# Raw weights asked for one chunk sooner, and a stick pair's first sigmoids and scan put behind the last begun weight chunk

## The chip, the cores and the metric

The kernel runs on one core of one Trainium2 chip. The metric is the device time of one execution in microseconds (us). The engines that matter here: TensorE (PE) multiplies, with its weight loads shown as PEld; VectorE (DVE) and ScalarE (ACT) work on elements; GpSimd (POOL) does little here but issue some transfers; SyncE (SP) only issues DMA transfers. Each of these takes its instructions in the order in which they were built, and waits in place where one is not ready.

## The reference

One decoder layer for a sequence of 512 tokens of width 1024, all in float32. Cut to what matters:

```python
h = rms_norm(x, norm_w)
qa, ka, va, za, qb, kb, vb, zb, gl_a, gl_b = split(h @ w_in)     # 8 x 512 columns, 2 x 1024
oa = moba_attention(rms_norm(qa), rms_norm(ka), va, rel_bias)    # 8 heads: scores, bias, softmax, values
ob = stick_breaking_attention(qb, kb, vb)                        # 8 heads, see below
ya = (oa * silu(za)) @ w_up_moba
yb = (ob * silu(zb)) @ w_up_sb
y  = sigmoid(gl_a + b_a) * ya + sigmoid(gl_b + b_b) * yb
x  = x + y @ w_out
```

A stick-breaking head weights key s of query t with sigmoid(z_ts) times the product of (1 - sigmoid(z_tj)) over the keys j between s and t. The product is a running one along a row, and is made with a scan instruction.

## The kernel before

**Three products for one.** Each float32 operand is split into a high part, which the matmul takes at full rate, and a low rest. A product is three matmuls: low by high, high by low, high by high (`mm3`, L225 to L227). Weights come as *chunks* of 128x1024 elements (512 KB). For each chunk SP issues the transfer into a raw tile `wr` (L170); ACT copies it to the high part `wh` (L179); DVE subtracts, which gives the low part `wl` (L181). There are three raw tiles and three each of `wh` and `wl`, used in turn, so chunk c's transfer waits until chunk c-3 is split, and chunk c's split until PE has used chunk c-3.

**Which chunk when.** `load_w` hands out chunks in the order of `stream` and keeps three fetched ahead: taking chunk c writes down transfer and split of chunk c+2. In the middle of the kernel the chunks go: 43 `zb:0`, 44 `za:3`, 45 `k:2`, 46 `g:9` (a block of gate logits), 47 `zb:1`, 48 `g:10`, 49 `k:3`, 50 `zb:2`, 51 `g:11`, 52 `up:0`, 53 `zb:3`. A tile carries its chunk's number: `wl48` belongs to chunk 48. A chunk of this kind is 24 matmuls of 512 columns.

**The pairs.** The loop over `PAIRS` (m = 0 to 7) handles two heads at a time: four pairs of branch a (softmax heads 0 to 7), then four of branch b (stick heads). For pair m it computes the scores of both heads on PE (L504), the weighted sum of pair m-2 (L594, evicted by DVE as `oa`, L599, then split into `oha` and `ola`), and then, for each head, turns scores into weights and stores them; between these stand the `FILLS`, the chunks that give PE work meanwhile: three to a pair here. A softmax head (`softmax`) is a bias add and minimum on DVE (L524), four exponentials on ACT (L526), scaling on DVE, three transposes on DVE (L566), four stores to DRAM from SP (`put`, L573, `pda6` for head 6) and one load back from ACT's queue (`get`, L580). A stick head (`stick`) has, for each of three row groups, two sigmoids on ACT (`om` = 1 - weight, L541, and `pb`, L542; L550 and L551 for the short rows), a scan on DVE (`sx`, L544, L554), a product (L546, L556), then the same transposes, stores (`pdb`) and load. Results of chunks of kind g are evicted by a sigmoid on ACT (L621), kind z by a sigmoid and a product (L607, L608), kind k by a split (L412, L413). They use two banks named `pj` in turn, with the weighted sums.

**What sets the order.** A scheduler in the tile layer places the instructions of each engine from its own estimate of when they are ready; `tc.issue_after(x)` adds that a row may stand only behind row x. Before, a stick head's first sigmoids are held behind the last gate eviction:

```python
with tc.issue_after(evicted[-1]):
    A.activation(om[:, S - n:S], sc[i], AF.Sigmoid, scale=-1.0)
```

The functions that the diff touches, and what calls them:

Of the kernel before, what the change touches and what calls it, by code (L numbers as in the profile page):

```python
# [9 lines left out]
F32 = mybir.dt.float32  # L10
F32R = mybir.dt.float32r
BF16 = mybir.dt.bfloat16
AF = mybir.ActivationFunctionType
ALU = mybir.AluOpType
AX = mybir.AxisListType

P = 128
S = 512
# [40 lines left out]
def hybrid_layer(ctx: ExitStack, tc: tile.TileContext, x, xT, w, rel, out):  # L59
    nc = tc.nc  # L60
    V, A, G, T = nc.vector, nc.scalar, nc.gpsimd, nc.tensor
# [3 lines left out]
    wp = ctx.enter_context(tc.tile_pool(name="wp", bufs=3))  # L65
# [29 lines left out]
    nw, mb, qw, kw = sm[:, 0:8], sm[:, 8:24], sm[:, 24:25], sm[:, 25:26]  # L95


    ahead, low, sums = [], {}, {}
    turn_of = cp.tile([1, 1], F32, name="turn_of")
    WO = w.shape[0] - len(BLOCKS)  # L100
    ORDER = {"v": ("11", "22", "T2", "21", "T3", "T1", "T4"), "q": ("11", "T1", "21", "T2", "22", "T3", "T4")}
# [3 lines left out]
    stream = list(range(8)) + list(range(20, 20 + len(FRONT))) + VOUT + QOUT + list(range(20 + len(FRONT), WO)) + OUT  # L105

    def block(name, kind):
        if kind == "q":
            return w[BASE[kind] + BLOCKS.index(name + "a") // 2]
        return w[BASE.get(kind, WO) + BLOCKS.index(name)]  # L110
# [38 lines left out]
    count = [0]  # L149

    def load_w():

        while len(ahead) < 3 and count[0] < len(stream):
            ahead.append(fetch_w(count[0]))
            count[0] += 1
        return ahead.pop(0)

    def fetch_w(c):
        cuts = ((0, 512), (512, 1024)) if c < 2 else ((0, 1024),)
        item = stream[c]  # L160
        if item in sums:
            raw = sums[item]
        else:
            src = w[item] if isinstance(item, int) else block(item[1], item[0]) if isinstance(item, tuple) else block(item, "o")
            raw = wp.tile([P, 1024], F32, tag="wr", bufs=3, name=f"wr{c}") if c else raw0
            for a, b in cuts:
                if a == 0 and 0 < c < 4:
                    raw_x(2 * c)
                if a or c:
                    nc.sync.dma_start(raw[:, a:b], src[:, a:b])  # L170
                if a == 0 and c < 4:
                    for k in (0, 1) if c == 0 else (2 * c + 1,):
                        raw_x(k)
        hi = wp.tile([P, 1024], F32R, tag="wh", name=f"wh{c}")
        lo = wp.tile([P, 1024], F32R, tag="wl", name=f"wl{c}")
        if c == 0:
            low[c] = load_x(0)
        for a, b in cuts:
            A.activation(hi[:, a:b], raw[:, a:b], AF.Copy)  # L179
            with tc.issue_after(low[0]) if c == 0 else nullcontext():  # L180
                low[c] = V.tensor_tensor(lo[:, a:b], raw[:, a:b], hi[:, a:b].bitcast(F32), op=ALU.subtract).ins  # L181
        return hi, lo
# [6 lines left out]
    def raw_x(k):  # L189
        if k == 0:  # L190
            xraw[k] = x0[:, SM:]
            nc.sync.dma_start(x0[:, SM + P:], xT[:, SM + P:SM + S])
        else:
            xraw[k] = slot(f"xr{k}")
            nc.sync.dma_start(xraw[k], xT[:, SM + k * S:SM + (k + 1) * S])
        if k == 4:
            nc.sync.dma_start(rb, rel)

    def load_x(k):
        raw = xraw[k]  # L200
        h = xp.tile([P, S], F32R, tag="xh", name=f"xh{k}")
        l = xp.tile([P, S], F32R, tag="xl", name=f"xl{k}")
        if k == 0:
            for cs in (slice(0, P), slice(P, S)):
                V.tensor_scalar(h[:, cs], raw[:, cs], nw[:, k:k + 1], None, op0=ALU.mult)
        else:
            A.activation(h, raw, AF.Copy, scale=nw[:, k:k + 1])
        last = V.scalar_tensor_tensor(l, raw, nw[:, k:k + 1], h.bitcast(F32), op0=ALU.mult, op1=ALU.subtract)
        xH.append(h)
        xL.append(l)  # L210
        return last.ins
# [91 lines left out]
    begin = cp.tile([P, S + P + 1], F32, name="begin")  # L303
# [70 lines left out]
    def load_bias(h):  # L374
        bt = oms[h % 2][:, :S]
        nc.sync.dma_start(bt, bass.AP(tensor=e_dr.tensor, offset=e_dr.offset + h * TW, ap=[[1, P], [1, S]]))
        return bt
# [115 lines left out]
    def scores(br, p, q, k, res):  # L493

        (qh, ql), (kh, kl) = q[p], k[p]
        for grp in ((3,), (2,), (1, 0)):
            ps = [bank("s", f"s{br}{2 * p + b}{grp[0]}") for b in range(2)]
            c = 0
            for i in grp:
                n = (i + 1) * P  # L500
                for m, (x, y) in enumerate(((qh, kl), (ql, kh), (qh, kh))):
                    for b in range(2):
                        o = slice(b * HD, (b + 1) * HD)
                        T.matmul(ps[b][:, c:c + n], x[o, i * P:(i + 1) * P], y[o, :n], start=m == 0, stop=m == 2)  # L504
                for b in range(2):
                    res[2 * p + b][i] = ps[b][:, c:c + n]
                c += n
            for b in range(2):
                res[2 * p + b][grp] = ps[b][:, :c]

    def row_tiles(br, h):

        p10 = tp.tile([P, 3 * P], F32, tag="p1", bufs=2, name=f"p{br}{h}1")
        return {3: tp.tile([P, S], F32, tag="p3", bufs=2, name=f"p{br}{h}3"),
                2: tp.tile([P, 3 * P], F32, tag="p2", bufs=2, name=f"p{br}{h}2"),
                1: p10[:, :2 * P], 0: p10[:, 2 * P:], (1, 0): p10}
# [15 lines left out]
    evicted = []  # L532

    def stick(h, sc, bias):

        rows = row_tiles("b", h)
        for i in (3, 2):
            n = (i + 1) * P
            om = oms[i - 2]
            with tc.issue_after(evicted[-1]):  # L540
                A.activation(om[:, S - n:S], sc[i], AF.Sigmoid, scale=-1.0)  # L541
            A.activation(rows[i], sc[i], AF.Sigmoid)  # L542
            sx = tp.tile([P, S], F32, tag="sx", bufs=2, name=f"sx{h}{i}")
            V.tensor_tensor_scan(sx[:, n - 1::-1] if n == S else sx[:, :n][:, ::-1], om[:, S + 1 - n:][:, ::-1],  # L544
                                 begin[:, S - n:S][:, ::-1], 0.0, op0=ALU.mult, op1=ALU.add)
            V.tensor_tensor(rows[i], rows[i], sx[:, :n], op=ALU.mult)  # L546

        z, p = (a.rearrange("p (n c) -> p n c", n=3) for a in (sc[1, 0], rows[1, 0]))
        with tc.issue_after(evicted[-1]):
            A.activation(short[:, :, :P], z, AF.Sigmoid, scale=-1.0)  # L550
        A.activation(p, z, AF.Sigmoid)  # L551
        n = 3 * (P + 1) - 1
        sx = tp.tile([P, S], F32, tag="sx", bufs=2, name=f"sx{h}1")
        V.tensor_tensor_scan(sx[:, :n][:, ::-1], short.rearrange("p n c -> p (n c)")[:, 1:][:, ::-1],  # L554
                             begin[:, S + P + 1 - n:][:, ::-1], 0.0, op0=ALU.mult, op1=ALU.add)
        V.tensor_tensor(p, p, sx[:, :n + 1].rearrange("p (n c) -> p n c", n=3)[:, :, :P], op=ALU.mult)  # L556
        return rows
# [178 lines left out]
    def split_o(br, p):  # L736
        u = ocol[br, p]
        oH[br, p] = slot(f"oh{br}{p}", F32R)
        oL[br, p] = slot(f"ol{br}{p}", F32R)
        A.activation(oH[br, p], u, AF.Copy)  # L740
        V.tensor_tensor(oL[br, p], u, oH[br, p].bitcast(F32), op=ALU.subtract)
# [62 lines left out]
    def fill(tag="pj"):  # L804

        for kind, i in fills.pop(0):
            home[0] = "s" if kind == "up" else tag
            make[kind](i)
# [7 lines left out]
    def finish(m, tag="s"):  # L816

        br, p = PAIRS[m]
        weighted(tag, br, p, v_of[br], [done.pop((m, b)) for b in range(2)])
        split_o(br, p)  # L820

    for m, (br, p) in enumerate(PAIRS):
        q, k = (qa, ka) if br == "a" else (qb, kb)
        sc = {h: {} for h in (2 * p, 2 * p + 1)}
        with tc.issue_after(end[0]):
            scores(br, p, q, k, sc)
        if m > 1:
            finish(m - 2, "pj")
        for b in range(2):
            h = 2 * p + b  # L830
            bias = load_bias(h) if br == "a" else None
            done[m, b] = put(br, h, turn(br, h, (softmax if br == "a" else stick)(h, sc[h], bias)))
            fill()
            if not b:
                done[m, 0] = get(*head(m, 0), done[m, 0])
        for b in range(2):
            if not b:
                done[m, 1] = get(*head(m, 1), done[m, 1])
            if (m, b) in SUMS:
                sum_w(SUMS[m, b], done[m, b])  # L840
            fill("pj" if (b or not fills[1]) and m < 7 else "s")
# [77 lines left out]
    for c in range(2):  # L919
        hi, lo = load_w()  # L920
# [83 lines left out]
```

## Time and profile before

| | |
|---|---|
| three runs | 389.46 us median (388.74 to 389.48) |
| profiled execution | 388.84 us, of which the span of the trace 387.1 |
| PE busy | 379.2 us (98%) |
| DVE, ACT, POOL busy | 290.3, 209.0, 79.4 us |
| granted TensorE clock, mean | 0.995 |
| transfers | 86.38 MB, mean 223 GB/s |

How to read it: the profile is one execution. A row of the timeline gives start, length, engine, source line, operation and tiles; in brackets stands how long the engine was idle before and what ended that. A row of the waits gives the waiting engine and line, what released it, total time, times, and the longest. The table of stretches gives, for a stretch of time, the busy time of each engine, the granted clock, the share of DMA time and the rate. Neighbouring rows of an engine overlap by some hundredths of a microsecond, so the distance between starts is the time that one row costs.

### The profile page before, as it was taken

How to read it: one execution, taken by the hardware profiler on the slowest of the kernel's cores; microseconds unless marked ns; L12 is line 12 of the kernel's file. 1: busy time of each engine (PE TensorE's matmuls, PEld its weight loads, DVE VectorE, ACT ScalarE, POOL GpSimd, SP SyncE). 2: the span in 40 equal slices, each digit the busy share in tenths (PEclk: the TensorE clock that was granted, in tenths of full speed). 3: DMA queues.
4: the chain of work that ended last, by engine and by line, in shares of the span. 5: the costliest groups of instructions: out<-in, count | busy, mean ns of one | idle time of the engine just before them, and what ended most of it. 6: DMA issues, size and time to landing. Idle time of an engine off the chain costs nothing.

```text
span 387.1 us, 5491 instructions
## 1 busy us (share of the span) xinstructions
PE 379.2 (98%) x1935; PEld 309.3 (80%) x1935; DVE 290.3 (75%) x503; ACT 209.0 (54%) x351; POOL 79.4 (21%) x124
## 2 busy tenths in 40 slices
PE   8999999999999999999999979999999999999996
PEld 5888888888888998887878757787877887888885
DVE  5838989925767469993989396598988834999963
ACT  6685566338664448772986470654553412358540
POOL 3959959020211100000000000010101000421310
PEclk9999999999999999999999998999999999999999
DMA  7989798994854745869677734769789781499955
GB/s 269 348 325 340 198 254 255 292 331 164 225 156 108 191 127 175 238 193 318 181 224 211 253 113 117 274 205 281 253 218 307 213 316 55 143 268 295 172 141 178
DMA packets 36747, 86.38 MB, mean 223 GB/s; under 512 B 3944, under 2 KB 16744, under 8 KB 36720
## 3 DMA queue, kind: packets, MB, share of 16 engines
q1 hardware_dynamic: 27696, 52.72, 41.8%
q0 software_dynamic: 6576, 22.57, 24.2%
q10 hardware_dynamic: 2448, 10.75, 8.2%
q8 instruction: 15, 0.25, 0.3%
q14 instruction: 12, 0.10, 0.1%
HBM read 67.65 MB, written 14.70 MB: 213 GB/s over the span
## 4 chain that ended last, share of the span: by engine, by line
PE 95%; DVE 2%; DMA 1%; issue 1%; ACT 0%; DVEq 0%; ACTq 0%
PE gl L226 8%; PE gl L227 8%; PE gl L225 8%; PE pob L594 2%; PE sa L504 2%; PE za L225 2%; PE yb L225 2%; PE yb L226 2%; PE ka L225 2%; PE za L226 2%; PE yb L227 2%; PE ya L226 2%; PE za L227 2%; PE vx L227 2%; PE ka L227 2%; PE kb L227 2%
## 5 line engine op out<-in xcount | busy, mean ns | idle before, releaser
L181 DVE TENSOR_TENSOR wl<-wr,wh 128x1024 fp32r<-128x1024 f32 (+1 forms) x61 | 71.7, 1179 | 31.8 <-ACT wh L179 31.4
L179 ACT ACTIVATE wh<-wr 128x1024 fp32r<-128x1024 f32 (+1 forms) x61 | 62.7, 1028 | 45.0 <-PE ya L227 12.0
L226 PE MATMUL gl<-xh,wl 128*128 128x512 f32 x128 | 50.7, 396 | 3.2 <-DVE wl L181 3.2
L225 PE MATMUL gl<-xl,wh 128*128 128x512 f32 x128 | 50.5, 394 | 0.0
L227 PE MATMUL gl<-xh,wh 128*128 128x512 f32 x128 | 50.4, 394 | 0.0
L140 POOL COPY turn_of<-ptb 1x1 f32<-1x1 f32 x3 | 1.8, 614 | 153.7 <-DMA ptb<-pdb 153.7
L226 PEld LDWEIGHTS gl<-xh,wl 128*128 128x128 f32 x128 | 24.4, 191 | 8.6 <-DVE wl L181 3.5
L225 PEld LDWEIGHTS gl<-xl,wh 128*128 128x128 f32 x128 | 24.4, 191 | 5.4 <-issue 0.4
L227 PEld LDWEIGHTS gl<-xh,wh 128*128 128x128 f32 x128 | 24.5, 191 | 5.1
L621 ACT ACTIVATE gl<-gl,x 128x512 f32<-128x512 f32 x16 | 11.0, 687 | 30.4 <-PE gl L227 29.6
L544 DVE TENSOR_TENSOR_SCAN sx<-om,begin 128x512 f32<-128x512 f32 (+1 forms) x16 | 17.2, 1080 | 6.9 <-ACT om L541 6.9
L526 ACT ACTIVATE pa<-pa,m 128x512 f32<-128x512 f32 (+3 forms) x32 | 17.6, 552 | 1.5 <-DVE m L524 1.3
L566 DVE STREAM_TRANSPOSE turnedb<-pb 128x384 f32<-128x384 f32 (+1 forms) x24 | 13.6, 599 | 0.1
L566 DVE STREAM_TRANSPOSE turneda<-pa 128x384 f32<-128x384 f32 (+1 forms) x24 | 13.6, 597 | 0.0
L524 DVE CUSTOM_DVE_ANT_0 pa<-sa,om 128x512 f32<-128x512 f32 (+3 forms) x32 | 13.5, 484 | 0.0
L225 PE MATMUL za<-xl,wh 128*128 128x512 f32 x32 | 12.9, 403 | 0.0
L225 PE MATMUL zb<-xl,wh 128*128 128x512 f32 x32 | 12.8, 400 | 0.0
L225 PE MATMUL yb<-olb,wh 128*128 128x512 f32 x32 | 12.6, 393 | 0.0
L226 PE MATMUL zb<-xh,wl 128*128 128x512 f32 x32 | 12.5, 390 | 0.0
L226 PE MATMUL za<-xh,wl 128*128 128x512 f32 x32 | 12.5, 390 | 0.0
L226 PE MATMUL yb<-ohb,wl 128*128 128x512 f32 x32 | 12.5, 390 | 0.0
L226 PE MATMUL ka<-wh,xl 128*128 128x512 f32 x32 | 12.5, 390 | 0.0
(428 smaller groups left out, 1065.2 us busy)
## 6 DMA issues: line engine op xcount, KB each, us to landing
wr<-in_w SPq DMA_DIRECT2D x57, 512.0 KB, 5.3
pda<-turneda SPq DMA_DIRECT2D x32, 160.0 KB, 2.8
pta<-pda ACTq DMA_DIRECT2D x8, 640.0 KB, 5.1
pdb<-turnedb SPq DMA_DIRECT2D x32, 160.0 KB, 3.1
ptb<-pdb ACTq DMA_DIRECT2D x8, 640.0 KB, 4.9
qT<-in_w POOLq DMA_DIRECT2D x6, 512.0 KB, 6.3
xn<-in_x SPq DMA_DIRECT2D x8, 256.0 KB, 6.3
om<-e_dr SPq DMA_DIRECT2D x8, 256.0 KB, 3.3
```

Of the source, the lines that this page charges most:

```text
L179: A.activation(hi[:, a:b], raw[:, a:b], AF.Copy)
L181: low[c] = V.tensor_tensor(lo[:, a:b], raw[:, a:b], hi[:, a:b].bitcast(F32), op=ALU.subtract).ins
L225: T.matmul(ps, aH, bL, start=start, stop=False, skip_group_check=on)
L226: T.matmul(ps, aL, bH, start=False, stop=False, skip_group_check=on)
L227: end[0] = T.matmul(ps, aH, bH, start=False, stop=stop, skip_group_check=on).ins
L504: T.matmul(ps[b][:, c:c + n], x[o, i * P:(i + 1) * P], y[o, :n], start=m == 0, stop=m == 2)
L524: V.tensor_tensor_reduce(rows[i], sc[i], bias[:, S - n:], scale=1.0, scalar=3e38, op0=ALU.add, op1=ALU.min, accum_out=m[:, 0, i:i + 1])
L526: A.activation(rows[i], rows[i], AF.Exp, bias=m[:, 0, i:i + 1], scale=-1.0, accum_out=m[:, 1, i:i + 1])
L544: V.tensor_tensor_scan(sx[:, n - 1::-1] if n == S else sx[:, :n][:, ::-1], om[:, S + 1 - n:][:, ::-1], begin[:, S - n:S][:, ::-1], 0.0, op ...
L566: V.transpose(turned[:, :, at:at + n, :].rearrange("p q j r -> p j q r"), rows[i].rearrange("p (j q c) -> p j q c", j=n, q=4))
L594: guard[0] = T.matmul(po[o, :].rearrange("p (a n r) -> p a n r", a=4, r=32)[:, :, i:i + n, :], vv[j][:, c:c + HD], src, start=j == NT - 1, ...
L621: evicted.append(A.activation(g, ps, AF.Sigmoid, bias=mb[:, i:i + 1]).ins)
```

## The change

Two edits, and what they need.

1. `load_w` issues, from the first pair on (`early`), the raw transfer of the next chunk as soon as three are ahead; `fetch_w` then takes the raw tile from `begun`. The split stays where it was in the program.
2. In `stick`, for the first head of a pair (h even), the sigmoids are held behind the last written `wh` (`split_of[0]`) instead of behind the last gate eviction, and the first scan behind its `wl` (`split_of[1]`). `high` and `low` keep those rows.

```diff
-    ahead, low, sums = [], {}, {}
+    ahead, low, high, sums = [], {}, {}, {}
...
         while len(ahead) < 3 and count[0] < len(stream):
             ahead.append(fetch_w(count[0]))
             count[0] += 1
+        c = count[0]
+        if early[0] and c < len(stream) and isinstance(stream[c], int):
+            begun[c] = wp.tile([P, 1024], F32, tag="wr", bufs=3, name=f"wr{c}")
+            nc.sync.dma_start(begun[c], w[stream[c]])
         return ahead.pop(0)
+
+    early, begun = [False], {}
 
     def fetch_w(c):
...
             raw = sums[item]
+        elif c in begun:
+            raw = begun.pop(c)
         else:
...
         for a, b in cuts:
-            A.activation(hi[:, a:b], raw[:, a:b], AF.Copy)
+            high[c] = A.activation(hi[:, a:b], raw[:, a:b], AF.Copy).ins
...
     def stick(h, sc, bias):
 
         rows = row_tiles("b", h)
+        split_of = high[count[0] - 1], low[count[0] - 1]
         for i in (3, 2):
             n = (i + 1) * P
             om = oms[i - 2]
-            with tc.issue_after(evicted[-1]):
+            with tc.issue_after(split_of[0] if h % 2 == 0 else evicted[-1]):
                 A.activation(om[:, S - n:S], sc[i], AF.Sigmoid, scale=-1.0)
             A.activation(rows[i], sc[i], AF.Sigmoid)
             sx = tp.tile([P, S], F32, tag="sx", bufs=2, name=f"sx{h}{i}")
-            V.tensor_tensor_scan(sx[:, n - 1::-1] if n == S else sx[:, :n][:, ::-1], om[:, S + 1 - n:][:, ::-1],
-                                 begin[:, S - n:S][:, ::-1], 0.0, op0=ALU.mult, op1=ALU.add)
+            with tc.issue_after(split_of[1]) if h % 2 == 0 and i == 3 else nullcontext():
+                V.tensor_tensor_scan(sx[:, n - 1::-1] if n == S else sx[:, :n][:, ::-1], om[:, S + 1 - n:][:, ::-1],
+                                     begin[:, S - n:S][:, ::-1], 0.0, op0=ALU.mult, op1=ALU.add)
             V.tensor_tensor(rows[i], rows[i], sx[:, :n], op=ALU.mult)
...
-        with tc.issue_after(evicted[-1]):
+        with tc.issue_after(split_of[0] if h % 2 == 0 else evicted[-1]):
             A.activation(short[:, :, :P], z, AF.Sigmoid, scale=-1.0)
...
+    early[0] = True
     for m, (br, p) in enumerate(PAIRS):
```

What the scheduler makes of it. PE's rows stand as before. The lines of the changed kernel are 8 to 10 higher (L181 becomes L189, L544 becomes L554).

*First stick pair (m = 4), DVE.* `wl` is a chunk's low part, `kb2l` and `qb2l` low parts of keys and queries, `sx03` the first scan of head 0, `sx12` and `sx11` scans of head 1, `oa2` and `ola2` the evicted weighted sum. Before, the rows at the first scan, and those at `wl48`:

```order
L181 TENSOR_TENSOR wl47_2191<-wr47_2188,wh47_2190 128x1024
L413 SCALAR_TENSOR_TENSOR kb2l_2220<-kb2_2194,kb2h_2219 128x512
L413 SCALAR_TENSOR_TENSOR qb2l_2224<-qb1_1260,qb2h_2223 128x512
L544 SCALAR_TENSOR_TENSOR sx03_2314<-om1_121,begin_108 128x512
L546 TENSOR_TENSOR pb03_2310<-pb03_2310,sx03_2314 128x512
```

```order
L544 SCALAR_TENSOR_TENSOR sx12_2382<-om0_120,begin_108 128x384
L554 SCALAR_TENSOR_TENSOR sx11_2387<-om_short_116,begin_108 128x386
L546 TENSOR_TENSOR pb12_2374<-pb12_2374,sx12_2382 128x384
L181 TENSOR_TENSOR wl48_2232<-wr48_2229,wh48_2231 128x1024
L741 TENSOR_TENSOR ola2_2306<-oa2_2303,oha2_2305 128x512
L181 TENSOR_TENSOR wl49_2339<-wr49_2336,wh49_2338 128x1024
```

Now, at the first scan, and at `wl49`:

```order
L189 TENSOR_TENSOR wl47_2191<-wr47_2130,wh47_2190 128x1024
L421 SCALAR_TENSOR_TENSOR kb2l_2222<-kb2_2196,kb2h_2221 128x512
L421 SCALAR_TENSOR_TENSOR qb2l_2226<-qb1_1260,qb2h_2225 128x512
L189 TENSOR_TENSOR wl48_2232<-wr48_2194,wh48_2231 128x1024
L554 SCALAR_TENSOR_TENSOR sx03_2316<-om1_121,begin_108 128x512
L556 TENSOR_TENSOR pb03_2312<-pb03_2312,sx03_2316 128x512
```

```order
L576 STREAM_TRANSPOSE turnedb0_2329<-pb02_2313 128x3x4x32
L576 STREAM_TRANSPOSE turnedb0_2329<-pb01_2311 128x3x4x32
L554 SCALAR_TENSOR_TENSOR sx13_2379<-om1_121,begin_108 128x512
L554 SCALAR_TENSOR_TENSOR sx12_2384<-om0_120,begin_108 128x384
L189 TENSOR_TENSOR wl49_2339<-wr49_2235,wh49_2338 128x1024
```

`wl48` moved from behind fifteen rows of the two heads to ahead of the first; `wl49` stands behind head 0's rows and two scans of head 1.

*The same place, ACT.* `pa73` to `pa71` are the exponentials of softmax head 7, `za3` the sigmoid of chunk 44, `gl9` the eviction of chunk 46, `om1` the first sigmoid of the stick pair. Before:

```order
L526 ACTIVATE pa71_2161,m7_2164<-pa71_2161,m7_2164 128x128
L580 DMA pta5_2013<-pda5_1975 128x1280
L179 ACTIVATE wh46_2126<-wr46_2124 128x1024
L607 ACT_TABLE_LOAD
L607 ACTIVATE za3_2155<-za3_2130 128x512
L179 ACTIVATE wh47_2190<-wr47_2188 128x1024
L412 ACTIVATE kb2h_2219<-kb2_2194 128x512
L412 ACTIVATE qb2h_2223<-qb1_1260 128x512
L580 DMA pta6_2158<-pda6_2119 128x1280
L621 ACTIVATE gl9_2260<-gl9_2235,x0_78 128x512
L541 ACTIVATE om1_121<-sb03_2262 128x512
```

Now:

```order
L617 ACTIVATE za3_2157<-za3_2132 128x512
L534 ACT_TABLE_LOAD
L534 ACTIVATE pa73_2164,m7_2166<-pa73_2164,m7_2166 128x512
L534 ACTIVATE pa72_2165,m7_2166<-pa72_2165,m7_2166 128x384
L534 ACTIVATE pa71_2163,m7_2166<-pa71_2163,m7_2166 128x256
L534 ACTIVATE pa71_2163,m7_2166<-pa71_2163,m7_2166 128x128
L187 ACTIVATE wh47_2190<-wr47_2130 128x1024
L420 ACTIVATE kb2h_2221<-kb2_2196 128x512
L590 DMA pta6_2160<-pda6_2121 128x1280
L420 ACTIVATE qb2h_2225<-qb1_1260 128x512
L187 ACTIVATE wh48_2231<-wr48_2194 128x1024
L631 ACT_TABLE_LOAD
```

`gl9` and `om1` follow. `wh48` stands ahead of the gate's sigmoid and the pair's; head 7's exponentials stand behind `za3` and no longer ahead of it, with a table load on either side; `wh46` has gone ahead of head 6's exponentials. On SP the transfer `wr48` now stands between the four stores `pda6` and the four stores `pda7`, before it stood behind both.

*Second stick pair (m = 5), DVE*, from its first scan to the eviction `oa3` of the last weighted sum of branch a. Before:

```order
L546 TENSOR_TENSOR pb22_2526<-pb22_2526,sx22_2534 128x384
L566 STREAM_TRANSPOSE turnedb2_2542<-pb22_2526 128x3x4x32
L181 TENSOR_TENSOR wl51_2437<-wr51_2434,wh51_2436 128x1024
L413 SCALAR_TENSOR_TENSOR qb3l_2470<-qb1_1260,qb3h_2469 128x512
L599 TENSOR_TENSOR oa3_2518<-poa3_2507,za3_2155 128x4x128
L554 SCALAR_TENSOR_TENSOR sx21_2539<-om_short_116,begin_108 128x386
```

Now:

```order
L556 TENSOR_TENSOR pb22_2528<-pb22_2528,sx22_2536 128x384
L421 SCALAR_TENSOR_TENSOR qb3l_2472<-qb1_1260,qb3h_2471 128x512
L564 SCALAR_TENSOR_TENSOR sx21_2541<-om_short_116,begin_108 128x386
L576 STREAM_TRANSPOSE turnedb2_2544<-pb22_2528 128x3x4x32
L566 TENSOR_TENSOR pb21_2526<-pb21_2526,sx21_2541 128x384
L554 SCALAR_TENSOR_TENSOR sx33_2594<-om1_121,begin_108 128x512
L609 TENSOR_TENSOR oa3_2520<-poa3_2509,za3_2157 128x4x128
```

`wl51` has moved out, to the end of the pair before; the short scan, a transpose, a product and head 3's first scan (`sx33`) have moved ahead of `oa3`.

## The prediction

> **What bounds the kernel now.** I read the page's header first, then PE's own waits, then a table of stretches cut at the starts of the pairs' scores.
>
> ```profile
> span 387.1 us, 5491 instructions
> PE 379.2 (98%) x1935; PEld 309.3 (80%) x1935; DVE 290.3 (75%) x503; ACT 209.0 (54%) x351; POOL 79.4 (21%) x124
> ...
> PE gl L226 <- DVE wl L181: 3.2, 1, 3.2
> PE pwarm L215 <- DVE warm L87: 1.0, 1, 1.0
> PE qa L273 <- ACT wh L179: 0.2, 1, 0.2
> ```
>
> PE is busy for 379.2 of 387.1 us, and it waits in one place that can be mended: once, 3.2 us, for a low weight part `wl` made by VectorE (DVE). The other two waits are at the start. The table of stretches, from one pair's scores to the next, shows what this wait costs in all:
>
> ```profile
> 198.13:219.05 20.92, 20.92 (x118) 16.57 (x117) 15.38 (x43) 11.99 (x25) 0.00 (x0) 1.00 0.88 282
> 219.05:245.12 26.07, 22.87 (x119) 17.71 (x118) 17.23 (x24) 10.87 (x19) 0.00 (x0) 0.93 0.48 144
> 245.12:266.04 20.92, 20.92 (x119) 16.57 (x118) 19.85 (x28) 11.48 (x20) 1.76 (x3) 1.00 0.72 215
> ...
> 232.66:236.16 3.50, 3.50 (x8) 2.82 (x9) 3.50 (x6) 0.00 (x0) 0.00 (x0) 0.51 0.11 29
> ```
>
> (Columns: stretch, its length, busy PE, PEld, DVE, ACT, POOL, granted clock, DMA share, GB/s.) Every pair holds the same PE work, one set of scores, one weighted sum, three chunks, and takes 20.92 us; the first stick pair takes 26.07. So 26.07 - 20.92 = 5.15 us are lost there: the wait, and behind it 3.5 us at a clock of 0.51. PE's rows in order of time:
>
> ```profile
> 229.00 0.46 PE L225 MATMUL gl<-xl,wh 128*128 128x512 f32 x1
> 232.66 0.80 PE L226 MATMUL gl<-xh,wl 128*128 128x512 f32 x1 [3.20 <-DVE wl L181]
> ```
>
> The first matmul of chunk 48 (gate block 10) runs on time, the second needs `wl48` and is 232.66 - 229.23 = 3.43 us late; at the slow clock the next eight take 3.50 where eight at 0.227 take 1.8, another 1.7. The two make 5.1. Why `wl48` is late is seen on DVE, ScalarE (ACT) and the SP queue:
>
> ```profile
> 214.96 0.68 DVE L413 SCALAR_TENSOR_TENSOR qb2l<-qb,qb2h 128x512 fp32r<-128x512 f32 x1
> 220.68 1.22 DVE L544 TENSOR_TENSOR_SCAN sx<-om,begin 128x512 f32<-128x512 f32 x1 [5.04 <-ACT om L541]
> ...
> 231.38 1.22 DVE L181 TENSOR_TENSOR wl<-wr,wh 128x1024 fp32r<-128x1024 f32 x1
> 233.11 1.22 DVE L181 TENSOR_TENSOR wl<-wr,wh 128x1024 fp32r<-128x1024 f32 x1
> ...
> 219.16 0.69 ACT L621 ACTIVATE gl<-gl,x 128x512 f32<-128x512 f32 x1 [4.32 <-PE gl L227]
> 227.00 1.06 ACT L179 ACTIVATE wh<-wr 128x1024 fp32r<-128x1024 f32 x1
> ...
> 207.05 4.80 SPq L573 DMA_DIRECT2D pda<-turneda  x8
> 211.95 1.81 SPq L170 DMA_DIRECT2D wr<-in_w  x3
> wr<-in_w SPq DMA_DIRECT2D x10, 512.0 KB, 5.2
> DMA to landing us min/median/max: 3.2/6.2/8.7
> ```
>
> DVE idles 5.04 us ahead of the scans and then runs fifteen rows of the two heads, 220.68 to 231.38, before `wl48`. ACT idles 4.32 us and makes `wh48` only at 227.00, behind twelve sigmoids of the heads. The raw chunk was asked for at 211.95, behind eight row stores of the heads; at the median of 5.2 it landed near 217.2. It was there while both engines idled: the order of work made the stall, not the amount.
>
> **The change part by part.** *PE* has the same 1866 rows in the same order, so nothing is added there; what can change is when a row's inputs are ready.
>
> *Raw transfer.* The built order puts `wr48` between the stores of heads 6 and 7 instead of behind both. Head 6's stores began at 207.05; now one weight part of 1.1 stands ahead of that head and head 7's bias rows no longer do, so I take 207.4 for them. Four stores at 4.80/8 = 0.60 us end at 209.8, the chunk lands at 209.8 + 5.2 = 215.0. That is only 2 us sooner; at the slowest landing of 8.7 it is 218.5. Elsewhere on SP a raw transfer has moved ahead of one or two heads' stores (`wr46` of heads 4 and 5, `wr51` of head 0): 0.6 us of issuing each, and the raw tile that it waits for is freed before those stores' rows are ready; PE wants what they carry a pair later, some 20 us. POOL's rows are the same.
>
> *ACT ahead of the pair.* Head 7's four exponentials now stand behind `za3`'s sigmoid, and with them come two more table loads:
>
> ```profile
> 204.01 0.71 ACT L526 ACTIVATE pa<-pa,m 128x512 f32<-128x512 f32 x1
> ...
> 206.20 1.04 ACT L179 ACTIVATE wh<-wr 128x1024 fp32r<-128x1024 f32 x1
> 207.26 1.28 ACT L607 ACT_TABLE_LOAD   x1
> 208.56 0.60 ACT L607 ACTIVATE za<-za 128x512 f32<-128x512 f32 x1
> ```
>
> `za3` is ready at about 208.1 (219.05, where the next scores start, less two chunks of 24 x 0.227 = 5.45 us), so: sigmoid to 208.7, table to 210.0, four exponentials 206.20 - 204.01 = 2.2 to 212.2, `wh47` 1.05 to 213.3, `kb2h` when its chunk ends at 213.6, `qb2h`, done near 214.9; `wh48` at the landing, 215.1 to 216.2, second table load to 217.5. The gate sigmoid cannot start before PE ends at 219.1, so this is hidden by 1.6 us. On DVE head 7 still has three transposes (0.61 + 0.50 + 0.50) and some short rows, about 2.5 from the exponentials' end: 214.7; then `wl47` 1.1, `kb2l`, `qb2l` 1.2, and `wl48` from 217.0 to 218.2. PE wants it at 229.2: 11 us ahead, where it was 3.4 behind. The whole 5.15 us at this place are gone, and with no gap nothing slows the clock. If the cover failed, each us of lateness over those 11 would cost a us.
>
> *Next in line: `wl49`* (chunk 49, wanted at 229.0 + 5.45 = 234.45). It stands behind head 0's whole work and two scans. From rows like those below: head 0's scans 1.32, 0.87, 0.87, its products 0.61, 0.55, 0.55, `oa2` 0.60, `ola2` 0.60, transposes 0.61, 0.50, 0.50, head 1's scans 1.13, 0.87, together 9.6; 220.7 + 9.6 + 1.1 = 231.4. Slack 3.0 us. Lower bound nothing, upper bound the rival below.
>
> *Next: the pair after it.* Here the order is tight. In time of the run before:
>
> ```profile
> 245.85 0.69 DVE L413 SCALAR_TENSOR_TENSOR kb3l<-kb,kb3h 128x512 fp32r<-128x512 f32 x1 [7.80 <-ACT kb3h L412]
> 246.75 1.22 DVE L544 TENSOR_TENSOR_SCAN sx<-om,begin 128x512 f32<-128x512 f32 x1 [0.20 <-ACT om L541]
> 248.07 0.69 DVE L546 TENSOR_TENSOR pb<-pb,sx 128x512 f32<-128x512 f32 x1
> 248.68 0.95 DVE L544 TENSOR_TENSOR_SCAN sx<-om,begin 128x384 f32<-128x384 f32 x1
> 249.55 0.69 DVE L566 STREAM_TRANSPOSE turnedb<-pb 128x512 f32<-128x512 f32 x1
> 250.16 0.52 DVE L546 TENSOR_TENSOR pb<-pb,sx 128x384 f32<-128x384 f32 x1
> 250.71 0.58 DVE L566 STREAM_TRANSPOSE turnedb<-pb 128x384 f32<-128x384 f32 x1
> 251.21 1.18 DVE L181 TENSOR_TENSOR wl<-wr,wh 128x1024 fp32r<-128x1024 f32 x1
> 252.32 0.68 DVE L413 SCALAR_TENSOR_TENSOR qb3l<-qb,qb3h 128x512 fp32r<-128x512 f32 x1
> 252.91 0.68 DVE L599 TENSOR_TENSOR oa<-poa,za 128x512 f32<-128x512 f32 x1
> 253.51 0.95 DVE L554 TENSOR_TENSOR_SCAN sx<-om_short,begin 128x386 f32<-128x386 f32 x1
> 254.38 1.20 DVE L181 TENSOR_TENSOR wl<-wr,wh 128x1024 fp32r<-128x1024 f32 x1
> ...
> 255.06 0.39 PE L225 MATMUL gl<-xl,wh 128*128 128x512 f32 x1
> ```
>
> PE's chunk 51 (gate block 11, at 255.06) writes the bank that `oa3` empties. Before, `oa3` ended at 253.5, 1.5 us ahead. Now `wl51` is out of the way, but the short scan, a transpose, a product and head 3's long scan stand in front: to 250.71 as shown, `qb3l` 0.59, short scan 0.87, transpose 0.50, product 0.55, scan 1.13 to 1.22, `oa3` 0.60 to 0.68 (with and without the 0.08 by which rows overlap): end between 254.95 and 255.1. So from 0.1 us early to 0.1 late; a wake-up of PE comes on top, and I take 0.1 us lost. Behind it a transpose 0.50, a product 0.61, `ola3` 0.60, a scan 0.87 and `wl52` 1.1 end 3.7 us later, near 258.7, and chunk 52 starts at 255.06 + 5.45 = 260.5: slack 1.8. Later pairs change places of a few rows; gate block 11's eviction there comes behind four sigmoids, which I cost at nothing since scores and a weighted sum still run on PE before its bank is wanted.
>
> The clock row above has 0.51 behind a delay of 3.43 us. The Trainium skill, page "TensorE: Matmul & The Clock Gate", section "What's actually happening", says that the clock halves after an idle window of about 3.4 us whose phase runs free. By that rule a short wait such as the one at chunk 51 would cost its own length alone, and the slow stretch before would be a matter of phase, so that the gain would lie between 3.4 and 5.15; here no shorter gap in mid-run shows it.
>
> **Sum.** The profiled execution took 388.84 (span 387.1 and 1.7 around it): 388.84 - 5.15 + 0.1 = 383.8. The median of the three runs is 389.46, 0.6 above, which gives 384.4; I predict **384.1**.
>
> **The rivals.**
> *The wait moves to chunk 51.* For it: DVE is busy for 19.85 of 20.92 us in that pair, and the slack just worked out is about nothing. Against: only one late scan could add more, since the chain restarts from PE's own `kb3`. One to two scans late (1.2 to 2.4 us): 385 to 386.5.
>
> *The change doesn't do what it says:* the stall only passes from chunk 48 to 49, since DVE has the same rows to do. For it: `wl49` is behind thirteen rows of the heads. Against: the stretch holds 17.23 us of DVE work, and 20.92 are enough for it. To lose all, `wl49` must be 3.0 + 5.15 = 8.2 us later than 231.4, or 3.0 + 3.4 = 6.4 if the clock falls again: 388.8.
>
> *Slower:* ACT takes its work in order, so `wh48`, waiting for the raw chunk, now blocks all sigmoids of the pair. Landing up to 216.6 is free (1.6 us); each us beyond delays the first scan, after 3.0 more PE waits at chunk 49, and from 1.6 + 3.0 + 5.15 = 9.75 us (landing at 224.8) the kernel is slower than before; at 12 us, 391. For it: the transfer stands behind head 6's stores, which depend on a longer DVE chain. Against: the slowest landing seen, 8.7, is 3.5 over the median.
>
> **How the numbers follow.** Forecast 0.75, own range 383.2 to 384.8 (the two bases, 0.4 either way for the runs' own spread of 388.74 to 389.48); wait at chunk 51 0.14; no gain 0.07; slower 0.04. The range reaches from 383.2 to 386.4, over the second case. What a measurement of this kernel can tell from no change is about 0.2%, 0.8 us: faster by more has the first two cases, 0.88 with a little off for their edge; within it 0.07; slower 0.05.
>
> **What would show it.** Right: PE's waits hold no `gl <- wl` row; every pair's stretch is 20.9 to 21.0 with clock 1.00; a `wl` row near 217 on DVE ahead of the first scan; two more table loads on ACT. Wrong: a PE row waiting for `oa` L609 or for a `wl` at chunk 49, a stretch above 21.5, or `wh48` starting later than 217.

## The result

| | before | after |
|---|---|---|
| executions | 389.28 us median (388.74 to 389.48) | 384.23 us median (383.77 to 384.35) |
| profiled execution, span | 387.1 | 382.4 |
| PE busy | 379.2 (98%) | 377.9 (99%) |
| granted TensorE clock, mean | 0.995 | 0.999 |

The ratio is 0.987, with a 95% interval of 0.9853 to 0.9887: 5.05 us less. A later comparison on one chip gave 384.96 us (383.88 to 387.59) against 389.22 (387.91 to 390.74), ratio 0.9896 (0.9864 to 0.9927); what is known of that wider spread is told with the experiments.

The profile after: header, PE's waits of 0.2 us or more, and the table of stretches, cut again where a pair's scores start (length, busy PE, PEld, DVE, ACT, POOL, granted clock, DMA share, GB/s).

```profile
span 382.4 us, 5493 instructions
PE 377.9 (99%) x1935; PEld 308.8 (81%) x1935; DVE 290.9 (76%) x503; ACT 211.3 (55%) x353; POOL 78.5 (21%) x124
...
PE pwarm L223 <- DVE warm L87: 1.0, 1, 1.0
```

```profile
198.54:219.46 20.92, 20.92 (x117) 16.57 (x117) 17.00 (x44) 15.57 (x28) 0.00 (x0) 1.00 0.76 232
219.46:240.38 20.92, 20.92 (x117) 16.58 (x117) 17.14 (x24) 10.75 (x19) 0.00 (x0) 1.00 0.64 202
240.38:261.35 20.97, 20.97 (x118) 16.52 (x118) 19.04 (x27) 10.41 (x19) 1.81 (x3) 1.00 0.73 223
```

The wait for `wl` is gone, and only the one at the start is left. In each of the three stretches PE is busy throughout at clock 1.00; the first stick pair does in 20.92 us what took 26.07, and the next takes 20.97. The scores of the first stick pair start 0.41 us later than before (219.46 for 219.05). All of that arises in the first 27 us, where PE's first four matmuls of `qa` take from 4.76 to 6.32 us and took from 4.74 to 5.82 before; executions of the changed kernel differ there as well (below). So the two profiled executions are 5.15 - 0.41 - 0.05 = 4.69 us apart, 388.84 and 384.15. The rows of time that carry this, on SP, ACT and DVE around the first stick pair (PE's chunk 48 starts at 229.41 here):

```profile
207.63 2.05 SPq L583 DMA_DIRECT2D pda<-turneda  x4
209.78 0.39 SPq L159 DMA_DIRECT2D wr<-in_w  x1
...
215.20 1.05 ACT L187 ACTIVATE wh<-wr 128x1024 fp32r<-128x1024 f32 x1
216.27 1.28 ACT L631 ACT_TABLE_LOAD   x1
219.57 0.69 ACT L631 ACTIVATE gl<-gl,x 128x512 f32<-128x512 f32 x1 [2.02 <-PE gl L235]
...
217.45 1.22 DVE L189 TENSOR_TENSOR wl<-wr,wh 128x1024 fp32r<-128x1024 f32 x1
221.09 1.22 DVE L554 TENSOR_TENSOR_SCAN sx<-om,begin 128x512 f32<-128x512 f32 x1 [2.43 <-ACT om L550]
...
230.37 1.20 DVE L189 TENSOR_TENSOR wl<-wr,wh 128x1024 fp32r<-128x1024 f32 x1
```

The raw chunk is asked for at 209.78, its high part is made at 215.20 and its low part at 217.45, 11 us ahead of its use, in time in which ACT still idles for 2.02 us and DVE for 2.43. `wl49` ends at 231.57.

### The profile page after: what moved, and what is told of

It is laid out like the page before. It is cut to its first block, busy times and chain, and to the rows that moved or that the text cites. A ratio compares the mean times of both kernels' runs of the same rounds, so it can differ in the third digit from the quotient of the medians.

```text
span 382.4 us, 5493 instructions
## 1 busy us (share of the span) xinstructions
PE 377.9 (99%) x1935; PEld 308.8 (81%) x1935; DVE 290.9 (76%) x503; ACT 211.3 (55%) x353; POOL 78.5 (21%) x124
## 4 chain that ended last, share of the span: by engine, by line
PE 99%; DVE 0%; issue 0%
PE gl L233 8%; PE gl L234 8%; PE gl L235 8%; PE poa L604 2%; PE pob L604 2%; PE sb L512 2%; PE sa L512 2%; PE za L233 2%; PE zb L233 2%; PE yb L233 2%; PE za L234 2%; PE zb L234 2%; PE yb L234 2%; PE ka L234 2%; PE ka L233 2%; PE kb L234 2%
## 5 line engine op out<-in xcount | busy, mean ns | idle before, releaser
L189 DVE TENSOR_TENSOR wl<-wr,wh 128x1024 fp32r<-128x1024 f32 (+1 forms) x61 | 71.8, 1181 | 31.6 <-ACT wh L187 31.5
L234 PE MATMUL gl<-xh,wl 128*128 128x512 f32 x128 | 49.9, 390 | 0.0
L140 POOL COPY turn_of<-ptb 1x1 f32<-1x1 f32 x3 | 0.7, 245 | 147.9 <-DMA ptb<-pdb 147.9
L554 DVE TENSOR_TENSOR_SCAN sx<-om,begin 128x512 f32<-128x512 f32 (+1 forms) x16 | 17.0, 1078 | 4.5 <-ACT om L550 4.5
```

Of the source, the lines that this page charges most:

```text
L234: T.matmul(ps, aL, bH, start=False, stop=False, skip_group_check=on)
```

## The experiments

The theory of the prediction (A) is that the place of chunk 48's split in the order made the stall, and that nothing but its place had to change. Its rivals are named in each expectation.

### Either edit alone

The first kernel keeps the early raw transfer and has the holds of `stick` as before:

```diff
-            with tc.issue_after(split_of[0] if h % 2 == 0 else evicted[-1]):
+            with tc.issue_after(evicted[-1]):
...
-            with tc.issue_after(split_of[1]) if h % 2 == 0 and i == 3 else nullcontext():
+            with nullcontext():
...
-        with tc.issue_after(split_of[0] if h % 2 == 0 else evicted[-1]):
+        with tc.issue_after(evicted[-1]):
```

> The changed kernel without the second edit: a stick pair's first sigmoids and scan are held as before, only the raw transfer is asked for one chunk sooner. In the built order the split of chunk 48 still stands ahead of the first sigmoid and the first scan, and all rows up to the end of the second stick pair are those of the changed kernel. Theory A (the gain comes from the split of chunk 48 standing in the idle time of ACT and DVE ahead of the first stick pair, whatever puts it there): the whole gain, 384.2 us (383.6 to 384.9), no wait of PE on the low weight part, the first stick pair's stretch 20.9 us. Theory B (the two holds of the second edit are what makes the gain): 389.3 us as before, with the 3.2 us wait, stretch 26.1 us.

Measured: 387.4 us median of executions from 384.59 to 389.38, ratio 0.9946 (0.9916 to 0.9976). In the profiled one (384.74), one of PE's waits, and the stretch of the first stick pair (cut at the times of the kernel before; from scores to scores, 219.24 to 240.16, it is 20.92 too):

```profile
PE sb L512 <- DVE gl L769: 0.2, 1, 0.2
...
219.05:239.97 20.92, 20.92 (x118) 16.59 (x116) 17.14 (x24) 10.76 (x19) 0.00 (x0) 1.00 0.63 202
```

At the disputed place theory A holds: the holds are not needed there, since the scheduler puts the split ahead by itself once it expects the chunk earlier. But A's time was only reached by some executions: five of twelve took 384.6 to 385.6, one 386.7, and six 388.1 to 389.4, five of these at a mean clock of 0.994 to 0.996. The expectation of 383.6 to 384.9 was a miss on that count.

The second kernel has the holds and not the early transfer:

```diff
-    early[0] = True
```

> The changed kernel without the first edit: the raw chunk 48 is asked for behind both heads' row stores as before (near 212 us, landing near 217), the holds stay. In the built order the split of chunk 48 now stands ahead of the stick sigmoids, but on ACT behind the gate's eviction and on DVE behind the evicted weighted sum oa2. Theory A (only the place of the split counts): high part made at 220.2 to 221.3 us, oa2 ends near 224.6 us, low part ready near 225.8 us, still 3.8 us ahead of PE's second matmul of chunk 48 at 229.6; first scan near 226 instead of 220.7, low part of chunk 49 ready near 233.5 against 235.1 wanted; second stick pair's scans 1.5 us later, which costs 0.1 to 0.4 us at chunk 51: 384.3 to 385.2 us. Theory C (the chunk must also be asked for sooner): PE waits again for the low part at chunk 48 or 49, 387 to 389.5 us.

Measured: 391.99 us (390.07 to 393.44), ratio 1.0075 (1.0049 to 1.01), slower than before by some 2.8 us (389.17 beside it). First its two `wl` rows of chunks 48 and 49, then PE's waits, then rows on SP and ACT and a stretch, one pair and more later:

```profile
224.58 1.22 DVE L189 TENSOR_TENSOR wl<-wr,wh 128x1024 fp32r<-128x1024 f32 x1
...
232.22 1.18 DVE L189 TENSOR_TENSOR wl<-wr,wh 128x1024 fp32r<-128x1024 f32 x1
```

```profile
PE zb L233 <- ACT wh L187: 3.4, 1, 3.4
PE ya L234 <- DVE wl L189: 1.0, 1, 1.0
...
PE zb L234 <- DVE wl L189: 0.5, 1, 0.5
```

```profile
251.19 10.63 SPq L583 DMA_DIRECT2D pdb<-turnedb  x8
261.92 11.87 SPq L178 DMA_DIRECT2D wr<-in_w  x5
...
269.38 1.06 ACT L187 ACTIVATE wh<-wr 128x1024 fp32r<-128x1024 f32 x1 [4.08 <-DMA wr<-in_w]
...
270.43:277.26 6.83, 6.31 (x14) 4.64 (x15) 6.79 (x9) 6.64 (x14) 1.46 (x2) 0.50 0.77 259
```

The stall at chunk 48 is gone here too, and the two low parts come when theory A said (224.58 to 225.8 and 232.22 to 233.4). Yet the kernel loses it all again: the first scan is at 226.3 and the heads' rows are later, PE waits 1.05 us at chunk 52 for a low part, and in this order the raw transfer of chunk 53 stands behind all eight stores of heads 2 and 3. The last four of these wait for their transposes until 258.3 and are issued by 261.8; the chunk's high part is made at 269.38, PE waits 3.38 us for it at chunk 53, and 6.83 us at half clock follow. So neither A's time (384.3 to 385.2) nor rival C's place (chunk 48 or 49) came true. With the holds in place the early transfer is needed, but not for the stall that it was to mend: with it the first scan is at 221.09, and the raw chunks ahead of heads 2 and 3 are issued by 241.5, before those stores.

### A late raw chunk

These two have both edits and put the raw transfer of chunk 48 behind the stores of heads 6 and 7, one with ten transfers of 8 elements into an unused tile between (as shown; `puts` holds the stores), one with none:

```diff
-            nc.sync.dma_start(begun[c], w[stream[c]])
+            after = puts[-1:]
+            for _ in range(10 if c == 48 else 0):
+                with tc.issue_after(after[-1]):
+                    after.append(nc.sync.dma_start(pad, w[stream[c]][:1, :8]).ins)
+            with tc.issue_after(after[-1]) if c == 48 else nullcontext():
+                nc.sync.dma_start(begun[c], w[stream[c]])
```

> Both edits, but the raw transfer of chunk 48 is put behind both heads' row stores and ten small transfers of 8 elements (an unused tile; the results don't change). In the built order the hold now puts all sigmoids of the first stick pair behind this late split, and the split itself stands behind the eviction of the weighted sum and of chunk 47 (zb1, whose PE work ends near 229.1 us). Theory A with its price for the slower rival: high part made near 229.7 to 230.8 us, low part near 232, so PE waits some 2.5 us at chunk 48; first scan at 232 instead of 220.7, so the low part of chunk 49 is ready near 238 to 239 where PE wants it near 237.2, then chunk 50 about 2 us late: in all 6 to 8 us over the changed kernel, 390 to 392.5 us, slower than before. Theory D (a late raw chunk costs only its own lateness, some 4 us of landing, against a slack of 11): 384 to 385 us.

Measured: 405.84 us (405.11 to 407.16), ratio 1.0438 (1.0398 to 1.0477).

```profile
217.77 13.48 SPq L163 DMA_DIRECT2D pad<-in_w  x10
231.30 6.34 SPq L165 DMA_DIRECT2D wr<-in_w  x4
...
234.97 1.06 ACT L193 ACTIVATE wh<-wr 128x1024 fp32r<-128x1024 f32 x1 [4.90 <-DMA wr<-in_w]
235.93 0.58 ACT L556 ACTIVATE om<-sb 128x512 f32<-128x512 f32 x1
```

The ten small transfers took 1.35 us each, so the high part was made at 234.97 where 229.7 was expected. The mechanism of the prediction's slower rival is plain in the rows: the pair's first sigmoid stands behind `wh48` and starts at 235.93. Theory D is out. The expected 390 to 392.5 was far too low: the chunk was later than reckoned, later pairs waited too, and the profile shows 20.5 us at a clock of 0.50 behind the waits, which none of the sums had.

> Both edits, but the raw transfer of chunk 48 is put behind the row stores of both heads 6 and 7 and nothing else: issued near 217.7 us where the changed kernel has it at 209.8, landing near 223 (at the median of 5.2). The built order has the high part of chunk 48 behind the split of the weighted sum (near 225.2 to 226.3 us) and ahead of all sigmoids of the first stick pair, so the first scan starts near 227.5 instead of 220.7. Prediction's price (each us of landing beyond 216.6 + 3.0 costs one us): 3.2 us, 387.5 us. By the rows of the kernel with the ten small transfers (first scan to the end of chunk 49's low part 7.1 us): low part of chunk 48 ready at 227.5 against 229.6 wanted, of chunk 49 at 234.6 against 235.1 wanted, so no wait in that pair; the next pair then is 2 to 3 us late and waits at chunks 51 and 52 by 1 to 2 us: 385 to 387 us. Theory D (late raw within the slack of 11 us costs nothing): 384.2 us.

Measured: 397.1 us (396.24 to 399.15), ratio 1.0207 (1.0177 to 1.0237); all three expected times were misses. PE's waits, late rows of SP, and the stretch behind the second of these waits:

```profile
PE gl L239 <- ACT wh L193: 2.7, 1, 2.7
PE sb L518 <- DVE gl L776: 2.4, 1, 2.4
PE ya L240 <- DVE wl L195: 1.7, 1, 1.7
...
306.71 4.60 SPq L589 DMA_DIRECT2D pdb<-turnedb  x4
311.41 9.75 SPq L165 DMA_DIRECT2D wr<-in_w  x5
...
289.08:292.50 3.42, 3.42 (x24) 2.18 (x22) 3.38 (x5) 0.87 (x2) 0.00 (x0) 0.50 1.00 373
```

`wl48` ended at 227.6 and `wl49` at 234.6, as worked out, and the first stick pair lost 0.5 us, at chunk 49 and not for its low part. The loss came later, some 12 us in all over the changed kernel in the same comparison (384.96) where the price of the prediction gave 3.2: at chunk 52 (1.72 us, 258.4), at the last pair's scores (2.43, 288.7) and at a gate chunk (2.66 and 0.76, 318.2 and 319.5) whose raw transfer was issued at 311.41, behind stores that waited for the late heads. Behind the second and the last of these the clock is at 0.50 for 3.4 us each, which costs another 3.4 us. So 6.4 us of lateness in the heads (first scan 227.53 for 221.09) are not paid once, where they first meet PE: later pairs pay again. That SP's order of stores and raw chunks does it is shown for the last of these waits alone.

### What a wait of PE costs

To see whether a wait costs its own length or more, and whether chunk 51 has slack, one DVE row was put directly ahead of `oa3` in the changed kernel. It reads the bank n times over:

```diff
+            hold = tc.issue_after(V.tensor_reduce(pad, po.unsqueeze(1).to_broadcast([P, n, S]), axis=AX.X, op=ALU.add).ins)
+        with hold:
```

> The changed kernel with one added DVE row directly ahead of the eviction oa3 of the second stick pair: a reduction that reads the weighted sum's bank twice over (1024 elements per partition, its result is not used). It delays the bank that PE's chunk 51 waits for. From the 512-element rows of DVE (0.5 to 0.6 us) I take 1.1 to 1.2 us. Slack theory (chunk 51 has no slack left, as the prediction worked out): PE waits for oa at chunk 51 by about 1.0 to 1.2 us. Clock: theory E (any wait of PE in mid-run halves the granted clock for 3.5 us): stretch 20.97 + 1.1 + 1.7 = 23.8 us, 387 us. Theory F (a short wait costs its own length alone, as by the Trainium skill, page TensorE: Matmul and The Clock Gate, section What's actually happening): stretch 22.1 us, clock 1.00, 385.3 us.

> As the kernel with 1024 elements, with 2048: 2.1 to 2.3 us of delay. Theory E (any wait halves the clock): stretch 20.97 + 2.2 + 1.7 = 24.9 us, 388.1 us. Theory F (short waits cost their length): 23.2 us, clock 1.00, 386.4 us.

> As before with 3072 elements: 3.2 to 3.4 us of delay, near the 3.2 us wait of the kernel before, which was followed by 3.5 us at a clock of 0.51. Theory E: stretch 20.97 + 3.3 + 1.7 = 26.0 us, 389.2 us. Theory F (a matter of phase near 3.4 us): either 24.3 us and 387.5 us with clock 1.00, or 26.0 us with a stretch at half clock.

> As before with 4096 elements: 4.3 to 4.5 us of delay, longer than the wait of the kernel before. Both theories expect the clock to halve: 20.97 + 4.4 + 1.7 = 27.1 us or, if the slow stretch lasts a whole further window, 1.7 more; 390.3 to 392 us. A stretch of 25.4 us at full clock would speak against both.

Measured: medians 385.19, 386.81, 389.16 and 392.4 us; ratios 0.9908 (0.9894 to 0.9921), 0.9944 (0.9925 to 0.9964), 1.0005 (0.9985 to 1.0025), 1.0094 (1.0018 to 1.0169). The added row and PE's wait in the kernels with n = 2, 4, 6 and 8, and the stretch behind the wait for n = 6:

```profile
249.50 1.21 DVE L612 TENSOR_REDUCE pad<-poa 128x2 f32<-128x1024 f32 x1
...
251.45 0.47 PE L234 MATMUL gl<-xl,wh 128*128 128x512 f32 x1 [0.88 <-DVE oa L614]
```

```profile
250.06 2.27 DVE L612 TENSOR_REDUCE pad<-poa 128x4 f32<-128x2048 f32 x1
...
253.07 0.47 PE L234 MATMUL gl<-xl,wh 128*128 128x512 f32 x1 [1.95 <-DVE oa L614]
```

```profile
249.54 3.34 DVE L612 TENSOR_REDUCE pad<-poa 128x6 f32<-128x3072 f32 x1
...
253.63 0.47 PE L234 MATMUL gl<-xl,wh 128*128 128x512 f32 x1 [3.02 <-DVE oa L614]
...
254.32:257.31 2.99, 2.99 (x9) 2.31 (x7) 2.99 (x5) 1.37 (x2) 0.86 (x1) 0.50 0.77 187
```

```profile
249.19 4.41 DVE L612 TENSOR_REDUCE pad<-poa 128x8 f32<-128x4096 f32 x1
...
254.34 0.48 PE L234 MATMUL gl<-xl,wh 128*128 128x512 f32 x1 [3.86 <-DVE oa L614]
```

| n | DVE delay, from start to start | pair, scores to scores | lost over 20.97 | beyond the delay |
|---|---|---|---|---|
| 2 | 1.12 | 22.07 | 1.10 | 0 |
| 4 | 2.19 | 23.16 | 2.19 | 0 |
| 6 | 3.25 | 25.82 | 4.85 | 1.60 |
| 8 | 4.31 | 26.66 | 5.69 | 1.38 |

Two things follow. Chunk 51 has no slack: what is put ahead of `oa3` comes back on PE to 0.02 us. And in these profiles a wait costs its length alone up to some 2 us, and from 3 us another 1.4 to 1.6 for the half clock behind it. (With n = 8 one matmul of chunk 52 stands ahead of the wait on PE, and the median is 0.4 us over the expected range.) It is also a matter of chance. With n = 4, four executions took 386.6 to 387.0 at a mean clock of 1.00, and two 387.9 at 0.996; with n = 6, one took 387.6 at 0.999 and seven 388.7 to 389.9 at 0.995 or 0.996. Two waits of nearly one length in other profiles show the same: behind the one of 2.43 us at 288.7 above the clock is at 0.50, behind one of 2.50 us in the n = 2 kernel (at 376.94, below) it stays at 1.00. This is theory F in the main, and the rule of the Trainium skill (page "TensorE: Matmul & The Clock Gate", section "What's actually happening") that the window runs free agrees with the chance. Its figure of a whole idle window of about 3.4 us does not fit the waits of 2.43 and 3.02 us that were followed by a half clock. For the two executions with n = 4 and a lower mean clock there is no row of time, only the mean.

### Where the spread comes from

> The changed kernel itself once more, beside the other runs here. The times of the kernel with the early raw chunk alone ran from 384.6 to 389.4 us, those of the kernel before from 387.7 to 390.9. Theory G (the spread is in the end of the program, which all these kernels share: a load of residual rows stands on SP behind two stores that wait for POOL's adding transfers, and in the profile of one kernel it came 5.5 us late for DVE): the changed kernel has the same spread, most runs near 384.2 and some at 386 to 389 us. Theory H (the spread belongs to the order that the early raw alone makes in the last two pairs): the changed kernel stays within 383.7 to 384.8 us.

Measured: 383.88, 384.39, 384.49, 385.44, 386.02 and 387.59 us. So the changed kernel has a spread of its own, and H is out as it was put. G is not shown by that alone. G came from a row of the n = 2 kernel, whose profiled execution took 388.15 where the eight others took 384.95 to 385.55:

```profile
375.33 0.42 DVE L929 TENSOR_TENSOR xres<-ox,xres 128x256 f32<-128x256 f32 x1 [5.45 <-DMA xres<-in_x]
...
376.94 0.50 PE L234 MATMUL ox<-wl,yh 128*128 128x512 f32 x1 [2.50 <-DVE wl L190]
```

Two kernels move that load of residual rows ahead of the stores that held it back, one with both edits, one with the early transfer alone:

```diff
     r12 = residual(0, 1)
+    r21 = residual(1, 0)
...
-    r21 = residual(1, 0)
```

> The changed kernel, with the load of the residual rows for the third output block written behind that for the second, so that on SP it stands ahead of the two stores of the first block. PE's order is the same. Theory G: no wait of DVE for the residual rows in the end, all runs within 383.6 to 384.8 us, 384.1 in the middle. Theory H: the same times as the changed kernel has beside it, spread and all.

Measured: 385.91 us (384.05 to 389.35), ratio 0.9916 (0.9882 to 0.995).

> The same move of the residual load in the kernel that has the early raw chunk alone, whose runs were 384.6 to 389.4 us. Theory G: the runs above 386 us are gone, median 384.0 to 384.8 us, so that the first edit alone has the whole gain. Theory H: runs from 384.6 to 389.4 as before the move, median 386 to 388 us.

Measured: 386.71 us (384.05 to 389.0), ratio 0.9934 (0.9907 to 0.996). The spread stays in both, so theory G falls as the main cause: the late residual load is one event, seen once.

The profile of the repeated changed kernel (385.44 us) is 1.29 us over the first (384.15). Of that, 0.57 arises in the first 27 us (the first stick pair's scores start at 220.03 and 219.46). The rest is another event. Its rows at the third stick pair, and behind them those of the first profile of the changed kernel (384.15):

```profile
251.18 9.28 SPq L583 DMA_DIRECT2D pdb<-turnedb  x8
...
265.90 0.33 ACTq L590 DMA_DIRECT2D ptb<-pdb  x1
266.28 0.69 ACT L631 ACTIVATE gl<-gl,x 128x512 f32<-128x512 f32 x1 [1.53 <-DMA pdb<-turnedb]
...
267.02 0.50 PE L233 MATMUL zb<-xl,wh 128*128 128x512 f32 x1 [0.68 <-ACT gl L631]
```

```profile
250.61 9.91 SPq L583 DMA_DIRECT2D pdb<-turnedb  x8
...
264.25 0.33 ACTq L590 DMA_DIRECT2D ptb<-pdb  x1
264.63 0.69 ACT L631 ACTIVATE gl<-gl,x 128x512 f32<-128x512 f32 x1 [0.43 <-issue]
...
265.73 0.50 PE L233 MATMUL zb<-xl,wh 128*128 128x512 f32 x1
```

Gate block 11's eviction stands on ACT behind the load of head 3's turned rows, which can only be issued when that head's stores have landed. PE's chunk 53 writes the bank that this eviction empties. In the first profile the eviction ended at 265.3, 0.4 us ahead; in the other the stores, issued by 260.5 us in both, landed 1.65 us later, and PE waited 0.68. The last kernel takes the eviction out from behind the load (and keeps the moved residual load):

```diff
-        nc.scalar.dma_start(pt, dr)
+        with tc.issue_after(evicted[-1]) if (br, h) == ("b", 3) else nullcontext():
+            nc.scalar.dma_start(pt, dr)
```

> The changed kernel with the moved residual load and one more move: on ACT the eviction of gate block 11 now stands ahead of the load of head 3's turned rows, which waits until that head's stores have landed. PE's order is the same. Theory K (in the changed kernel that eviction stands behind this load with 0.3 to 0.5 us of slack before PE's chunk 53 needs the bank; a late store then makes PE wait, 0.7 us in one profile, and that is the spread of the runs above 385 us): no wait of PE for a gate eviction, the eviction ends 1 us ahead of chunk 53, runs within 383.7 to 385.0 us, median 384.1. Theory L (the spread is of another cause, or of several): runs from 384 to 389 us as with the moved residual load alone, median 385 to 386.

Measured: 384.55 us (384.2 to 384.99), ratio 0.9881 (0.9861 to 0.9901). All five executions lie within 0.8 us. Its profile shows what the move does:

```profile
251.46 9.49 SPq L583 DMA_DIRECT2D pdb<-turnedb  x8
...
264.91 0.71 ACT L632 ACTIVATE gl<-gl,x 128x512 f32<-128x512 f32 x1
268.75 0.33 ACTq L591 DMA_DIRECT2D ptb<-pdb  x1
...
266.57 0.50 PE L233 MATMUL zb<-xl,wh 128*128 128x512 f32 x1
```

In this execution the stores, issued by 260.95, let the load go only at 268.75, and PE has no wait. In the order of the changed kernel the eviction would have ended near 269.8 and PE would have waited 3.2 us; that wait is worked out, not measured. Theory K holds for this event. That the event is the main cause of the spread is not shown: these five executions ran on another chip than the six of the changed kernel and the seven with the moved residual load, the changed kernel was not run beside them, and its first four executions (383.77 to 384.35) lie as close together without this move. It is no faster than the changed kernel at its best; by the rows it gives up less when a store is late. Whether the executions of the early-transfer kernel above 388 us are the same event was not settled: there all sigmoids of that pair's first head stand behind this eviction and both loads, but its two profiled executions (384.74 and, with the moved residual load, 385.13) do not have the wait, and this last move was not tried in it. Both lose 0.8 us at another place, the last pair's scores, where PE waits for a row of DVE (L769) and the changed kernel's profiles show no wait; five of the six and all three of their executions at 388 us and more also show a mean clock of 0.994 to 0.996, as the kernels do in which PE waits 3 us.

## Why the prediction was right, point by point

- **The 5.15 us.** Right in place and size in the profile compared: 26.07 became 20.92. That it is 3.43 of lateness and 1.7 of clock is borne out by the kernel before itself: of 19 of its executions on one chip, five took 387.8 to 388.1 at a mean clock of 0.999, twelve 388.9 to 389.7 at 0.995 or 0.996, and two 390.2 and 390.9; between the first two groups lie some 1.4 us. So some 3.6 us of the gain do not hang on the clock (387.8 against 384.23), and the rest is the clock that most executions of the kernel before lose.
- **The sum, and luck in it.** For the profiled execution it gave 383.8; measured were 384.15, because 0.41 us were lost in the first 27 us, on which it had no term, and 0.05 instead of 0.1 at chunk 51. The median of 384.23 came from four executions, none above 384.35. The six of the later comparison have a median of 384.96, above the upper end of the range of 384.8; that none of the first four was slow is luck, and the forecast owes part of its closeness to it. (The count of 1866 PE rows stands in no profile; both profiles count 1935 matmuls.)
- **Raw transfer, ACT and DVE ahead of the pair.** Issue 209.8 (measured 209.78), `wh48` 215.1 (215.20), `wl48` done at 218.2 (218.67), the gate sigmoid not held up, with 2.0 us of idle time where 1.6 was reckoned, since PE was 0.4 later.
- **`wl49`.** 231.4 (231.57).
- **Chunk 51.** 0.1 us lost was taken from a range of -0.1 to 0.1. The pair took 20.97, 0.05 more than its neighbours, and the added rows show that there is indeed no slack.
- **Gate block 11 behind four sigmoids, "which I cost at nothing".** This step failed, though not in the executions first compared. The four sigmoids are harmless; what the step overlooked is the load issue that also stands ahead, with a slack of 0.4 us against stores that let the load go 3.7 us after they were issued in one profile and 7.8 us after in another (264.25 - 260.52 and 268.75 - 260.95). It cost 0.68 us in one profile.
- **The rival "slower".** The mechanism is real: 397.1 and 405.84 us. Its price was too low, because it counted each us of lateness once, at chunk 49, and put the break-even at a landing of 224.8. With the first scan 6.4 us later that price gives 384.1 + 6.4 - 3.0 = 387.5; measured were 397.1, with 0.5 us lost at chunk 49 and the rest in later pairs, 3.4 of it to the clock, for which the price had no term. The scan was late there because ACT had `wh48` behind the split of the weighted sum (225.29, the chunk had landed at 223.2), not for the landing itself.
- **The clock rule.** Weighed in the prediction as giving a gain between 3.4 and 5.15. Waits of 1 us did cost their length alone; the wait of 3.2 us was long enough to lose the clock in most executions.

## What to carry to other kernels

Where a wait shows on the engine that bounds the kernel, look for idle time of the engines that feed it just ahead: work that was ready then and stood behind other rows can be moved ahead, which cost nothing here. Before moving a row behind another, list every row that now stands between them, transfers' issues included, and give each its latest time as seen, not its usual one. An order with a slack of some tenths of a microsecond behind a transfer cost nothing in one execution and 0.7 us in the next, and a third store was late enough for 3.2, so look at the spread of the executions too.

## What the runs showed that was not expected

- Lateness multiplied here: 6.4 us at the first scan became some 12 us in all (397.1 against 384.96), 3.4 of them at half clock.
- A delay of 2.19 us cost PE 2.19 us, one of 3.25 us cost 4.85 (n = 4 and n = 6). A wait of 2.43 us was followed by a half clock, another of 2.50 us was not.
- The last store of a head took 3.7 us until the load behind it could go in one execution, 5.4 and 7.8 us in two others, with the same stores ahead of it.
- Removing one edit of a pair turned a gain of 5 us into a loss of 2.8 (391.99 against 389.17), most of it at a place two pairs away from the one that it mends.
